# Taking out a 128-byte tile that shifts the feed-forward operand slots against the weights

## The chip, the cores and the metric

The kernel runs on one core of a Trainium2 chip. The metric is the device time of one execution in microseconds (us). Before the change it was 1255.39 us, the median of three runs (1254.78 to 1256.69).

A core has a matrix engine (TensorE, PE in the profile, with its weight loads listed apart as PEld), a vector engine (VectorE, DVE), a scalar engine (ScalarE, ACT), a general one (GpSimd, POOL) and a queue processor (SyncE, SP). Data lies in SBUF, an on-chip memory of 128 partitions; a tile takes the same range of bytes in each of them, so its place is one address. TensorE reads both of its operands from SBUF and writes its sums to another memory, PSUM.

## The reference

The program is a decoder trunk of two layers on 512 tokens of 1,024 channels, in float32, one sequence:

- layer 0 mixes the tokens with attention: 3 groups of 8 heads, causal windows of 128, 512 and 2,048 tokens with strides 1, 4 and 16 and a linear bias, merged by their softmax denominators;
- layer 1 mixes them with causal means over 2, 4, 8 and 16 tokens, each in a quarter of the channels, with a matrix product before and one after;
- each layer then has a feed-forward network, `(silu(h @ gate) * (h @ up)) @ down`, with 2,816 hidden channels;
- there is a root-mean-square norm ahead of each of these and one at the end; the outputs are added to the stream.

## The kernel before

Activations are kept transposed: a tile holds 128 channels on its partitions and the 512 tokens along them (2,048 bytes). A product takes a block of 128 x 128 weights as the stationary operand and streams 512 or 256 columns of activations past it.

**Three products for one.** Each float32 value is split in a rounded part and a remainder (`split`, line 95: `hi` on ScalarE, `lo` on VectorE), both in the type float32r. Every product is then three matmuls, weights hi by activations hi, hi by lo, and lo by hi (lines 272, 273 and 275 in `Product.add`; lines 391 to 393 in `mult`). A pair of hi and lo tiles of 512 columns each, 4,096 bytes together, is what the kernel calls a slot.

**Seven products for eight.** Most of the large products are done by a Strassen scheme of 2 x 2 blocks, with 256 columns to a matmul: `seven` (line 400) and `values12` in attention, `chain` (line 449) in the feed-forward layers. A `chain` goes through its seven block products in a written-out order; each is `n` blocks of 128 by three matmuls. The last of the seven uses a half-size weight tile (`halfhi`, `halflo`) and adds to a sum that was evacuated before. The other products, the "plain" ones, stream all 512 columns: the first five of the 22 hidden blocks of each feed-forward layer (`plain_pair`), the pooling mixer, the output product of attention and some others.

**Where operands lie.** Pools are laid out in SBUF one behind the other. The first, `cpool`, holds the residual stream x, some small tiles and 12 slots; `wpool` holds the raw weights as they land from memory and the split weights; `tmp` holds small temporary tiles. Behind these, one range is used three times over: for the attention pools (`opool`, `apool`), and when they are closed for `fpool` with 16 further slots and, behind it, the scratch pools of the feed-forward layers and of the pooling mixer.

Slots are handed out by a queue. `slot` (line 283) takes the first free number and makes a tile under the tag of that number, in whichever pool the number belongs to; `give` (line 290) puts a number at the queue's end:

```
    free, pools = deque(range(FIXED)), {i: cpool for i in range(FIXED)}

    def slot(name, dtype=F32R):
        i = free.popleft()
        t = pools[i].tile([P, 2, S], dtype, tag=f"slot{i}", name=name, bufs=1)
        return i, t
```

In attention only numbers 0 to 11 exist (`FIXED = 12`); the other operands lie in tiles of the attention pools. When `fpool` opens, numbers 12 to 27 (`SLOTS = 16`) join the queue, and from then on an operand, whatever its name (`h`, `tb`, `tt`, `tn`, `hx`, `hy`, `hz`, `hu`, `n`, `y`), lies in either pool, as the queue has it. Weights always lie in `wpool`, but for those of the pooling mixer's second product (`wg`), which are in slots.

**What sets the order.** One queue of weight loads and one of splits are worked off by `pump` (line 186), which is called between the products, so a split for a later product stands between the evacuations of earlier ones. The order of all instructions is fixed when the program is built, and so is every address.

**Two tiles named shift.** Neither is ever written or read. One, of 256 bytes, is the first of `tmp` (line 89). The other, of 128 bytes, is the first of `fpool` (line 922), ahead of the slots.

Of the kernel before, what the change touches and what calls it, by code (L numbers as in the profile page):

```python
# [8 lines left out]
F32 = mybir.dt.float32  # L9
# [6 lines left out]
P = 128  # L16
# [35 lines left out]
def trunk(ctx: ExitStack, tc: tile.TileContext, xT, norms, w_first, w_qk, w_qkp, w_v0, w_v0p, w_v12, w_out, w_pair, w_down, w_down0, w_down1, w_down2, w_pin, w_pgrp,  # L52
# [866 lines left out]
                note(1, m)  # L919

    with tc.tile_pool(name="fpool", bufs=1) as fpool:
        fpool.tile([P, 32], F32, name="shift", bufs=1)
        for i in range(FIXED, FIXED + SLOTS):
            free.append(i)
            pools[i] = fpool
# [445 lines left out]
```

## Time and profile before

| | |
|---|---|
| median of three runs | 1255.39 us |
| the profiled execution | 1255.31 us, of it 1253.5 us span |
| TensorE (matmuls / weight loads) | 1238.3 us / 1173.6 us busy, 9,072 each |
| VectorE | 1012.8 us busy |
| ScalarE | 679.9 us busy |
| GpSimd | 157.7 us busy |
| granted TensorE clock | 0.998 |
| read from HBM | 186.29 MB, 150 GB/s over the span |

The span is the time between the first and the last instruction that was recorded. Roughly, attention lies in the first 460 us, its output product behind it, the first feed-forward layer from 510 to 835, the pooling mixer and the plain products of the second feed-forward layer from 835 to 957, and the rest of that layer from there to 1242; the norm at the end follows. A matmul's duration in the profile is modelled and reaches into the next one's; what one of them costs in a stream is the distance from its start to the next start.

### The profile page before, as it was taken

The page shows a single profiled execution, that of the slowest core. Times are in us where ns is not written, and L with a number is a line of the kernel's source. Part 1 is how long each engine was busy: PE and PEld are TensorE (multiplying, and loading weights), DVE is VectorE, ACT ScalarE, POOL GpSimd, SP SyncE. Part 2 cuts the span into 40 slices and gives each one's busy share as a digit, 9 for nine tenths or more (in the row PEclk, how much of TensorE's full clock was granted, in tenths as well). Part 3 has the DMA queues.
Part 4 walks back from the last instruction along what each step waited for, and adds up shares of the span by engine and source line. Part 5 has one row for each costly group of instructions (what it writes and reads, how often), then busy time and mean ns, then how long its engine had stood idle before and what let it go on. Part 6 is the DMA issues. An engine that isn't in the chain of part 4 may idle for free. (4 is left out here: it accounts for less than half of the span.)

```text
span 1253.5 us, 23247 instructions
## 1 busy us (share of the span) xinstructions
PE 1238.3 (99%) x9072; PEld 1173.6 (94%) x9072; DVE 1012.8 (81%) x1687; ACT 679.9 (54%) x1171; POOL 157.7 (13%) x147
## 2 busy tenths in 40 slices
PE   9999999999999999999999999999999999999997
PEld 7889999999999998889999999988788999999997
DVE  7987787878778747698778888798989877888876
ACT  6444554445455535466466556554446646656652
POOL 1111111111111010101111111100220111111100
PEclk9999999999999999999999999999999999999999
DMA  8336556655755443437777687553144777677742
GB/s 280 109 92 171 136 143 149 165 133 146 186 141 140 138 152 119 109 94 184 184 186 170 177 191 178 137 198 123 51 118 100 190 189 179 147 192 205 169 123 68
DMA packets 76719, 189.91 MB, mean 151 GB/s; under 512 B 7600, under 2 KB 15936, under 8 KB 76608
## 3 DMA queue, kind: packets, MB, share of 16 engines
q1 hardware_dynamic: 51696, 142.26, 35.8%
q0 software_dynamic: 24336, 45.63, 22.2%
q8 instruction: 71, 1.16, 0.4%
q10 hardware_dynamic: 576, 0.52, 0.1%
q14 instruction: 40, 0.33, 0.1%
HBM read 186.29 MB, written 2.10 MB: 150 GB/s over the span
## 5 line engine op out<-in xcount | busy, mean ns | idle before, releaser
L96 ACT ACTIVATE whi<-raw 128x1024 fp32r<-128x1024 f32 (+2 forms) x315 | 318.7, 1016 | 254.0 <-PE seed L392 78.5
L97 DVE TENSOR_TENSOR wlo<-raw,whi 128x1024 fp32r<-128x1024 f32 (+2 forms) x315 | 366.6, 1167 | 108.0 <-ACT whi L96 107.2
L158 POOL DMA_DIRECT2D raw<-w_pair x34 | 41.1, 1209 | 312.3 <-DMA raw<-w_pair 61.9
L391 PE MATMUL sum<-tt,whi 128*128 128x256 f32 x272 | 77.0, 283 | 1.6 <-ACT seed L473 0.8
L392 PE MATMUL sum<-tt,whi 128*128 128x256 f32 x272 | 76.6, 282 | 0.0
L393 PE MATMUL sum<-tt,wlo 128*128 128x256 f32 x272 | 76.4, 281 | 0.0
L96 ACT ACTIVATE halfhi<-rawhalf 128x512 fp32r<-128x512 f32 (+1 forms) x87 | 53.1, 612 | 19.5 <-PE sum L392 12.2
L173 DVE TENSOR_TENSOR raw<-raw 128x512 f32<-128x512 f32 (+1 forms) x87 | 57.5, 661 | 1.8 <-issue 1.7
L174 DVE TENSOR_TENSOR raw<-raw 128x512 f32<-128x512 f32 (+1 forms) x87 | 57.5, 661 | 0.2
L97 DVE TENSOR_TENSOR halflo<-rawhalf,halfhi 128x512 fp32r<-128x512 f32 (+1 forms) x87 | 57.4, 661 | 0.0
L158 POOL DMA_DIRECT2D raw<-w_down x24 | 28.9, 1206 | 213.8 <-DMA raw<-w_down 75.4
L391 PEld LDWEIGHTS sum<-tt,whi 128*128 128x128 f32 x272 | 51.3, 189 | 2.0 <-ACT seed L473 1.0
L473 ACT COPY seed<-sum 128x256 f32<-128x256 f32 x58 | 20.8, 359 | 57.5 <-PE sum L393 56.3
L392 PEld LDWEIGHTS sum<-tt,whi 128*128 128x128 f32 x272 | 51.3, 188 | 0.0
L393 PEld LDWEIGHTS sum<-tt,wlo 128*128 128x128 f32 x272 | 51.2, 188 | 0.0
L391 PE MATMUL sum<-hz,whi 128*128 128x256 f32 x160 | 45.3, 283 | 0.5 <-ACT seed L473 0.3
L392 PE MATMUL sum<-hz,whi 128*128 128x256 f32 x160 | 45.2, 283 | 0.0
L392 PE MATMUL seed<-hy,whi 128*128 128x256 f32 x160 | 45.2, 282 | 0.0
L393 PE MATMUL seed<-hy,wlo 128*128 128x256 f32 x160 | 45.1, 282 | 0.0
L393 PE MATMUL sum<-hz,wlo 128*128 128x256 f32 x160 | 45.1, 282 | 0.0
L391 PE MATMUL seed<-hy,whi 128*128 128x256 f32 x160 | 45.0, 281 | 0.0
L158 POOL DMA_DIRECT2D raw<-w_qkp x18 | 22.0, 1222 | 166.9 <-DMA raw<-w_qkp 109.4
(610 smaller groups left out, 4628.3 us busy)
## 6 DMA issues: line engine op xcount, KB each, us to landing
raw<-w_pair SPq DMA_DIRECT2D x78, 512.0 KB, 4.8
raw<-w_qkp SPq DMA_DIRECT2D x36, 512.0 KB, 4.3
raw<-w_pair POOLq DMA_DIRECT2D x34, 512.0 KB, 7.7
raw<-w_down SPq DMA_DIRECT2D x32, 384.0 KB, 3.7
raw<-w_v SPq DMA_DIRECT2D x18, 512.0 KB, 4.0
raw<-w_qkp POOLq DMA_DIRECT2D x18, 512.0 KB, 7.3
rawhalf<-w_pair SPq DMA_DIRECT2D x34, 256.0 KB, 4.5
raw<-w_down SPq DMA_DIRECT2D x16, 512.0 KB, 4.7
```

Of the source, the lines that this page charges most:

```text
L96: nc.scalar.activation(hi, v, AF.Copy)
L97: nc.vector.tensor_tensor(lo, v, hi.bitcast(F32), op=OP.subtract)
L158: nc.gpsimd.dma_start(b.rearrange("p (a c) -> p a c", a=2), self.src[:, None, 3 * q:].to_broadcast([P, 2, q]), accum_op=OP.add)
L173: nc.vector.tensor_add(a[:, :q], a[:, :q], b[:, :q])
L174: nc.vector.tensor_add(a[:, q:2 * q], a[:, q:2 * q], a[:, :q])
L391: nc.tensor.matmul(dst, w.t[0][:, c], th, start=k == 0 and not onto, stop=False, skip_group_check=onto)
L392: nc.tensor.matmul(dst, w.t[0][:, c], tl, start=False, stop=False, skip_group_check=onto)
L393: nc.tensor.matmul(dst, w.t[1][:, c], th, start=False, stop=k == n - 1, skip_group_check=onto)
L473: nc.scalar.copy(e, c)
```

## The change

One line goes: the 128-byte tile at the head of `fpool`. The 16 slots and all tiles behind them (the scratch of the feed-forward layers and of the pooling mixer) lie 128 bytes lower. The instructions and their order are the same, and so is the hand-out of slot numbers.

```diff
     with tc.tile_pool(name="fpool", bufs=1) as fpool:
-        fpool.tile([P, 32], F32, name="shift", bufs=1)
         for i in range(FIXED, FIXED + SLOTS):
             free.append(i)
             pools[i] = fpool
```

## The prediction

> **What bounds the kernel now.** I read first the engines' busy time, then busy time stage by stage, then the waits of TensorE, and last the spacing of single matmuls. The first two:
>
> ```profile
> span 1253.5 us, 23247 instructions
> PE 1238.3 (99%) x9072; PEld 1173.6 (94%) x9072; DVE 1012.8 (81%) x1687; ACT 679.9 (54%) x1171; POOL 157.7 (13%) x147
> ...
> 75.00:450.00 375.00, 372.87 (x3030) 367.71 (x3029) 301.87 (x486) 191.78 (x345) 59.22 (x62) 1.00 0.60 153
> 530.00:835.00 305.00, 302.90 (x2399) 295.18 (x2398) 255.35 (x431) 183.76 (x319) 32.79 (x28) 1.00 0.66 166
> 835.00:950.00 115.00, 114.29 (x511) 91.68 (x510) 104.43 (x187) 54.36 (x81) 17.55 (x12) 1.00 0.37 108
> 950.00:1242.00 292.00, 292.00 (x2388) 288.62 (x2387) 237.98 (x413) 173.46 (x306) 32.16 (x27) 1.00 0.64 158
> ```
>
> The columns of the stage rows are time, then busy time with count of PE, PEld, DVE, ACT and POOL, the granted clock, and the DMAs. TensorE is busy throughout: 302.90 of 305.00 us in the first feed-forward layer, 292.00 of 292.00 in the second, always at clock 1.00. DVE has 50 us free in each of these stages. TensorE's waits in the first layer are these, and in the second the view names none:
>
> ```profile
> PE sum L391 <- ACT seed L473: 1.1, 2, 0.8
> PE sum L391 <- ACT seed L465: 1.0, 2, 0.8
> ```
>
> So the time is TensorE's stream of matmuls, and what counts is how far apart two of them start. The durations in the groups (about 280 ns for 256 columns) overlap and don't say that; the starts do. In time order:
>
> ```profile
> 582.31 0.28 PE L391 MATMUL seed<-tn,whi 128*128 128x256 f32 x1
> 582.32 0.19 PEld L392 LDWEIGHTS seed<-tn,whi 128*128 128x128 f32 x1
> 582.43 0.28 PE L392 MATMUL seed<-tn,whi 128*128 128x256 f32 x1
> 582.43 0.19 PEld L393 LDWEIGHTS seed<-tn,wlo 128*128 128x128 f32 x1
> 582.55 0.28 PE L393 MATMUL seed<-tn,wlo 128*128 128x256 f32 x1
> ```
>
> Starts are 0.12 us apart, and the load of the next weights begins with each matmul: TensorE reads two places of SBUF at once, the moving operand in its slot and the next weights. [...]
>
> **The change part by part.** It removes one allocation. No instruction, wait or DMA is added, removed or reordered. The tile is never written. From the tile sizes (small tiles take 32 bytes each) x, the 12 slots of the first pool, raws and weights all lie at one offset modulo 256; the temporary pool is a multiple of 256 long, so the attention pools start at that offset too, and so would the feed-forward pool, but for the 128 bytes. Today the 16 slots there are "displaced" by 128 against the weights; afterwards everything is "aligned". The scratch tiles behind the slots also move by 128 bytes; only DVE, ACT and POOL touch them, and those are hidden by the TensorE stream above (if that cover were gone, nothing in the trace gives them a price by offset).
>
> The trace already holds both layouts. In attention no displaced slot exists, so it is the control. In the feed-forward layers I followed the hand-out of slots through the free list, a queue. Stretches without a stall, 256 columns; the first four wholly aligned (three in attention, one in layer two), the last two wholly displaced:
>
> ```profile
> 98.68:118.71 20.04, 20.04 (x169) 1.00 0.55 131
> 159.66:172.49 12.83, 12.83 (x109) 1.00 0.52 120
> 343.91:350.99 7.08, 7.08 (x60) 1.00 0.66 131
> 1099.19:1104.22 5.03, 5.03 (x44) 1.00 0.46 122
> 640.81:643.66 2.85, 2.85 (x26) 1.00 0.28 106
> 1093.48:1098.12 4.63, 4.63 (x41) 1.00 0.58 101
> ```
>
> The count includes one or two matmuls still running at the left edge; 167, 107, 59, 42, 24 and 39 start inside. Aligned: 20.04/167 = 120.0 ns, 119.9, 120.0, 119.8. Displaced: 2.85/24 = 118.8 and 4.63/39 = 118.7. The aligned stream is the slower one by 1.2 ns, and the last and the fourth row stand next to each other in the same stage, 1 us apart. Why the long aligned runs come so close to 120 is seen just behind a stall in attention; the first row is the eight matmuls that follow it, the second begins two later:
>
> ```profile
> 300.92:301.87 0.95, 0.95 (x10) 1.00 0.88 134
> 302.11:304.99 2.88, 2.88 (x26) 1.00 0.49 87
> ```
>
> 0.95/8 = 118.8 at first, then 2.88/24 = 120.0: an aligned stream settles at 120, a displaced one stays where the aligned one begins. Next, stretches of the feed-forward stages in which the two kinds mix:
>
> ```profile
> 563.59:583.38 19.79, 19.79 (x168) 1.00 0.74 187
> 603.55:613.43 9.87, 9.87 (x85) 1.00 0.73 188
> 786.87:804.56 17.69, 17.69 (x150) 1.00 0.58 139
> 966.18:986.00 19.81, 19.81 (x168) 1.00 0.75 185
> 1086.49:1104.22 17.73, 17.73 (x150) 1.00 0.66 156
> 1104.59:1111.88 7.29, 7.29 (x62) 1.00 0.86 215
> 1187.52:1205.20 17.69, 17.69 (x151) 1.00 0.56 139
> ```
>
> With 167, 83, 149, 167, 149, 61 and 149 starts these are 109.87/925 = 118.8 ns, 118.5 to 119.5 each; the highest, 7.29/61, has the fewest displaced operands (13 of 61). So in the mix even the aligned matmuls run at 118.8: each switch of offset restarts the unsettled phase. After the change there is no switch left, and all of them lose it, not the displaced alone.
>
> Term one. The feed-forward stages hold 4,596 matmuls of 256 columns: per layer 17 block pairs of 7 x 4 x 3 = 84, and down blocks of 4 x 84 + 8 x 63, together 2,268; twice that, and 60 at the end. About 75 of them follow a stall, at present one per 60 matmuls, so the runs will be as long as the third and fourth aligned rows, which I take with a little less for the shorter ones: 119.85. 4,520 x (119.85 - 118.8) = **+4.7 us**. Bounds: 4,596 x (120.0 - 118.8) = +5.5 above, nothing below.
>
> Term two, the wide matmuls (512 columns). Aligned in attention and the start of layer one, then displaced in the pooling stage:
>
> ```profile
> 57.82:68.49 10.66, 10.66 (x48) 1.00 0.36 63
> 462.81:508.86 46.05, 46.05 (x204) 1.00 0.30 92
> 847.01:852.38 5.36, 5.36 (x24) 1.00 0.01 3
> 865.99:870.87 4.88, 4.88 (x22) 1.00 0.64 210
> 879.86:884.75 4.89, 4.89 (x22) 1.00 0.33 107
> ```
>
> With 47 and 203 starts: 226.8 and 226.9 ns. With 23, 21 and 21: 233.0, 232.4, 232.9. Here aligned is the faster one, by 6 ns. Displaced wide operands are 168 of the pooling layer's input h, 60 of n and 12 of y, 240 in all, from 841 to 957 us: 240 x 5.9 = 1.4 at most. Not all stand in such clean runs; I take **-1.3 us** (bounds -1.4 and 0). Wide matmuls are few because only five of 22 hidden blocks and the pooling layer use them; that is why the sign is that of term one.
>
> Term three, small stalls. The last product of a chain often waits some 40 to 100 ns for the evacuation before it:
>
> ```profile
> 583.26 0.28 PE L393 MATMUL seed<-tn,wlo 128*128 128x256 f32 x1
> 583.38 0.33 PE L391 MATMUL sum<-tt,halfhi 128*128 128x256 f32 x1
> 583.54 0.28 PE L392 MATMUL sum<-tt,halfhi 128*128 128x256 f32 x1
> ```
>
> Here the gap is 0.16 instead of 0.12 us. About 60 chains have it. The 12 matmuls in front will take 12 x 1.05 = 13 ns longer; if the evacuation isn't later for that, the stall shrinks by as much: 60 x 13 = 0.8 at most, nothing if it moves along. I take **-0.3 us**.
>
> Sum: +4.7 - 1.3 - 0.3 = +3.1. The profiled execution took 1255.3 us, its span 1253.5 and 1.8 around it; that is at the median of the three runs (1255.39). Forecast **1258.4 us**.
>
> A rule speaks against this. The Trainium skill, "TensorE: Matmul & The Clock Gate", section "Step-by-step: what each phase is for", says of TensorE's two read ports: "Loading the next tile's weights doesn't steal SBUF read bandwidth from the running matmul." By it the offset is worth nothing (the rival below). Its section "Back-to-back issue gap" gives N/2.4 + 2.5 ns, an estimate of 109 and 216 for 256 and 512 columns; the trace has 119 to 120 and 227 to 233, so something beyond streaming is paid here, and it differs with the offset.
>
> **The rivals.** *Ports don't interact* (or the slots don't move by the whole 128): the spacings above differ for another reason, say the stage. Then the time stays at 1255.3; if only the wide ones gain, 1254.0. For it: the 256-column difference is 1%. Against: the two adjacent rows at 1093 and 1099 us.
>
> *Faster*: aligned operands in the feed-forward chains stay in the unsettled, quick phase. There is such a piece, nine aligned matmuls behind a switch:
>
> ```profile
> 602.34:603.39 1.06, 1.06 (x11) 1.00 0.00 0
> ```
>
> 1.06/9 = 117.7 ns. If all ran so, 4,520 x (117.7 - 118.8) - 1.3 = -6.3, 1249 us. It decides from the point where the aligned mean in the two layers lies under 118.5. Against it stand the row from 1099.19 (119.8 in the same stage) and all of attention.
>
> *The whole loss*: stalls no longer unsettle the stream, term one is +5.5, and the wide matmuls, which stand beside other work, gain nothing: 1260.8.
>
> **How the numbers follow.** My forecast has 0.70, ports don't interact 0.15, the whole loss 0.10, faster 0.05. The forecast's own range is 1257.3 to 1259.6 by the bounds of its terms. The range for the time goes from 1254.6, which takes in an unchanged time and most of the small gain, to 1260.6. A measurement of this kernel tells about 0.2% (2.5 us) from no change, that is 1257.9 and above is slower. Of the forecast's 0.70 about 0.51 lies above that and 0.19 below; with the whole loss, slower has 0.61. Same: 0.19 + 0.14 = 0.33. Faster: 0.06, the faster rival and a hundredth of the first.
>
> **What would show it.** In the changed kernel's starts, stall-free stretches of 256 columns after 555 us should average 119.8 to 120.0 and settle at 120 exactly, as attention does; attention and the wide matmuls up to 510 us should not move; displaced wide ones should drop from 233 to 227. The first layer's stage should be some 2 us longer, the second's the same, the pooling stage some 1 us shorter. I am wrong if the 256-column spacing stays near 118.8, if new waits of TensorE of a microsecond appear, or if the pooling stage doesn't shorten.

## The result and the profile after

The changed kernel takes 1257.72 us, the median of 22 runs (1256.51 to 1259.48); the kernel before, over 22 runs, 1255.12 us (1254.11 to 1257.17). The ratio is 1.0019, 95% interval 1.0013 to 1.0024: slower by 0.19%, which is 2.4 us (the two medians differ by 2.6), and lies at the bound of 0.2% that the prediction set itself. The profiled execution has a span of 1256.6 us against 1253.5. Each ratio below is against runs of the kernel before on the same chip.

The head of the page after:

```profile
span 1256.6 us, 23247 instructions
PE 1240.2 (99%) x9072; PEld 1177.5 (94%) x9072; DVE 1012.9 (81%) x1687; ACT 679.8 (54%) x1171; POOL 157.5 (13%) x147
```

VectorE, ScalarE and GpSimd are where they were (1012.8, 679.9, 157.7 before). Only TensorE's numbers grew. Now by stage; the columns are as in the prediction, and each stretch begins and ends at the same matmul in both kernels: the first feed-forward layer, the pooling mixer with the wide products of the second layer, the rest of the second layer. Before:

```profile
515.21:835.08 319.87, 317.77 (x2464) 307.51 (x2463) 270.22 (x456) 192.96 (x333) 35.04 (x29) 1.00 0.66 164
835.08:957.09 122.01, 121.30 (x540) 97.41 (x539) 111.44 (x202) 57.91 (x88) 17.55 (x12) 1.00 0.39 110
957.09:1236.04 278.95, 278.95 (x2308) 276.94 (x2307) 226.39 (x385) 167.04 (x293) 31.34 (x26) 1.00 0.65 162
```

After:

```profile
514.14:835.49 321.35, 319.62 (x2464) 309.74 (x2463) 270.30 (x456) 193.01 (x333) 35.04 (x29) 1.00 0.66 163
835.49:956.53 121.04, 119.93 (x540) 97.30 (x539) 110.98 (x202) 57.74 (x88) 17.50 (x12) 1.00 0.39 111
956.53:1239.13 282.60, 280.92 (x2308) 278.98 (x2306) 226.56 (x386) 167.08 (x294) 31.34 (x26) 1.00 0.65 160
```

The layers got longer by 1.5 and 3.7 us, the wide stage shorter by 1.0. The seven mixed stretches of the prediction, cut at the same matmuls, after the change:

```profile
562.51:582.54 20.03, 20.03 (x168) 1.00 0.75 185
602.82:612.76 9.94, 9.94 (x85) 1.00 0.73 186
787.06:804.93 17.87, 17.87 (x151) 1.00 0.59 136
965.69:985.72 20.02, 20.02 (x168) 1.00 0.73 184
1086.86:1104.73 17.87, 17.87 (x151) 1.00 0.67 152
1105.10:1112.40 7.31, 7.31 (x62) 1.00 0.77 208
1190.27:1208.15 17.87, 17.87 (x151) 1.00 0.54 133
```

167, 83, 149, 167, 149, 61 and 149 matmuls start inside, 925 in all: 110.91/925 = 119.9 ns apart, where it was 118.8. The control in attention and two stretches of the wide matmuls, at the same places as before:

```profile
97.59:117.62 20.03, 20.03 (x169) 1.00 0.54 131
847.42:852.66 5.25, 5.25 (x24) 1.00 0.01 4
866.11:870.87 4.76, 4.76 (x22) 1.00 0.66 223
```

Attention stands still (20.03/167 = 120.0). The wide ones went from 233 to 5.25/23 = 228.2 and 4.76/21 = 226.7.

The order of the matmuls is the same in both kernels, so the distance to the next start can be subtracted matmul by matmul over all 9,072. Wide matmuls are counted as stalled from 245 ns, the others from 150 ns:

| from 515 us on | us |
|---|---|
| 256 columns, unstalled, first layer / second layer | +2.57 / +2.37 |
| 512 columns, unstalled | -1.4 |
| stalled, 256 columns, first layer / second layer | -1.04 / +1.30 |
| stalled, 512 columns | +0.4 |

Attention's first microseconds, which the change doesn't touch, were 1.1 us shorter in this profile. The sum is the 3.1 us by which the spans differ. What the stalls are is taken up behind the experiments.

### The profile page after: what moved, and what is told of

Read it like the earlier page. It is cut to its first block, busy times and chain, and to the rows that moved or that the text cites. A ratio compares the mean times of both kernels' runs of the same rounds, so it can differ in the third digit from the quotient of the medians.

```text
span 1256.6 us, 23247 instructions
## 1 busy us (share of the span) xinstructions
PE 1240.2 (99%) x9072; PEld 1177.5 (94%) x9072; DVE 1012.9 (81%) x1687; ACT 679.8 (54%) x1171; POOL 157.5 (13%) x147
```

## The experiments

My theory: TensorE reads the moving operand and the next weights at the same time, and the spacing of its matmuls follows from the offset of the two places modulo 256. The rivals are that the scratch tiles' new place does it, that the absolute address does, and that it is the switching between two offsets, not the offset.

**Scratch tiles put back.** The padding goes behind the slots.

```diff
-        fpool.tile([P, 32], F32, name="shift", bufs=1)
...
-        invcnt = fpool.tile([P, PAD], F32, name="invcnt", bufs=1)
+        invcnt = fpool.tile([P, PAD + 32], F32, name="invcnt", bufs=1)[:, :PAD]
```

> The changed kernel, with 128 bytes of padding behind the slots, so that the scratch tiles have the addresses of before while the slots stay aligned with the weights. Theory (slots against weights decide): as the changed kernel, 1257.7 us, ratio to before 1.002. Rival (the scratch tiles' new place slows VectorE or ScalarE and through them TensorE): as before, 1255.1, ratio 1.000.

Measured 1258.15 us, ratio 1.0022 (1.0013 to 1.0031). Two of the stretches from above, one with 256 columns (167 starts) and one wide (21):

```profile
563.07:583.09 20.02, 20.02 (x168) 1.00 0.74 185
866.54:871.30 4.76, 4.76 (x22) 1.00 0.71 240
```

119.9 and 226.7 ns, as in the changed kernel. The scratch tiles play no part that these runs can tell.

**256 bytes ahead of the slots.** `[P, 32]` becomes `[P, 64]`.

> The kernel before, with 256 instead of 128 bytes ahead of the slots: slots aligned modulo 256 again, but at another absolute address than in the changed kernel, and off by 256 modulo 512. Theory (only the offset modulo 256 counts): 1257.7 us, ratio 1.002. Rivals: the absolute address or the offset modulo 512 counts, then it is as before, 1255.1; or the removal of the allocation itself costs, then 1255.1 too.

Measured 1258.58 us, ratio 1.0025 (1.0015 to 1.0035). The same two stretches:

```profile
563.20:583.24 20.03, 20.03 (x168) 1.00 0.74 185
865.72:870.48 4.76, 4.76 (x22) 1.00 0.69 226
```

Equal again, with the slots 256 bytes away from where the changed kernel has them. It is neither the absolute address nor the offset modulo 512, and taking the allocation out costs nothing by itself.

**64 bytes ahead of the slots.** `[P, 32]` becomes `[P, 16]`.

> The kernel before, with 64 instead of 128 bytes ahead of the slots. Theory in its narrow form (a switch between two different offsets unsettles the stream, whatever they are): 1255.1 us, ratio 1.000, with 256 columns at 118.8 ns in the feed-forward stages. Rival (128 bytes are special, as half of 256): as aligned, 1257.7. The wide matmuls at 64 bytes may cost another price than at 128, 227 to 233 ns, worth up to 1.4 us.

Measured 1256.04 us, ratio 1.0008 (0.9999 to 1.0017), which doesn't tell it from the kernel before. The same two stretches, and between them one of 149 starts with 256 columns:

```profile
563.46:583.27 19.81, 19.81 (x168) 1.00 0.74 187
787.43:805.19 17.76, 17.76 (x150) 1.00 0.60 139
866.55:871.37 4.82, 4.82 (x22) 1.00 0.64 225
```

118.6, 119.2 and 229.5 ns. Taking the matmuls of the feed-forward stages by slot, those 64 bytes off had 118.1 and the aligned ones between them 120.4, more than they have alone. So a switch doesn't always help the aligned ones; it depends on the pair.

**Matmuls alone.** To have the price of each offset without the kernel around it, a program splits one set of weights and one moving tile as the kernel does and runs streams of the kernel's triples, the moving operand starting `o` bytes on:

```
    def run(n, triples, offs):
        ...
        for k in range(triples):
            e = offs(k) // 4
            c = slice(k % 8 * P, (k % 8 + 1) * P)
            h, l = mhi[:, e:e + n], mlo[:, e:e + n]
            nc.tensor.matmul(p, whi[:, c], h, start=k == 0, stop=False)
            nc.tensor.matmul(p, whi[:, c], l, start=False, stop=False)
            nc.tensor.matmul(p, wlo[:, c], h, start=False, stop=k == triples - 1)
```

> A program of matmuls alone, which computes nothing of the reference: one set of weights, split in hi and lo as in the kernel, is multiplied with one moving tile read from a start that is shifted by 0 to 512 bytes; 72 matmuls of 256 columns for each start, then 36 of 512 columns; also streams in which the start changes every 4 triples or every triple. Theory (the spacing of two starts depends on the moving operand's offset against the weights modulo 256): at shifts 0, 256 and 512 256 columns settle at 120.0 ns and 512 columns at 227; at 128 they take about 118.5 and 232; alternating 0 and 128 gives 118.8. Rival (the offset plays no part, the stage does): all shifts give one and the same spacing. What shifts that are no multiple of 128 give is open.

Streams of 256 columns at 0 (69 starts), 32, 64, 128 and 256 bytes (72 each), then of 512 columns at 0, 64 and 128 (36 each):

```profile
21.13:29.41 8.28, 8.28 (x71) 1.00 0.01 2
37.96:46.35 8.40, 8.40 (x74) 1.00 0.01 2
46.35:54.84 8.48, 8.48 (x74) 1.00 0.00 0
63.46:72.00 8.54, 8.54 (x74) 1.00 0.01 2
97.45:106.08 8.63, 8.63 (x74) 1.00 0.01 2
174.65:182.84 8.19, 8.19 (x38) 1.00 0.01 2
199.58:207.82 8.24, 8.24 (x37) 1.00 0.00 0
216.23:224.63 8.40, 8.40 (x37) 1.00 0.00 0
```

256 columns: 120.0 at 0, 116.7 at 32, 117.8 at 64, 118.6 at 128, 119.9 at 256. 512 columns: 227.5, 228.9, 233.3. The kernel's prices come out here too, where the place of the moving operand is all that differs from stream to stream. Streams that switch between 0 and 128 bytes every four triples came to 119.1 ns, and every triple to 118.8; the first of them (72 starts):

```profile
140.47:149.05 8.58, 8.58 (x74) 1.00 0.01 2
```

Its matmuls at 0 had 119.3, less than the 120.0 that they have alone: this pair does pull the aligned ones down. And neither the aligned place nor the one of before is the best: 32 and 64 are quicker for 256 columns, which most of the kernel has.

**All slots at one offset.** If so, all of cpool's and fpool's slots should get the same offset, in attention too. A tile of W words is put ahead of the weights, and F words stand ahead of the feed-forward slots; the attention pools, which hold wide operands, stay aligned with the weights.

```diff
     wpool = ctx.enter_context(tc.tile_pool(name="wpool", bufs=1))
+    wpool.tile([P, W], F32, name="apart", bufs=1)
...
-        fpool.tile([P, 32], F32, name="shift", bufs=1)
+        fpool.tile([P, F], F32, name="shift", bufs=1)
```

First 128 bytes (W 32, F 32), the test for the switches: every slot is displaced as fpool's were before, and none differs from another.

> The same with 128 in place of 32 bytes: every slot is displaced by 128 bytes against the weights, those of the first pool too, and no switch of offset is left in the feed-forward layers. Theory (displacement itself gives the spacing, 118.6): feed-forward 4,520 x (118.6 - 118.8) = -0.9, attention 2,391 x (118.6 - 119.85) = -3.0, wide +3.4: 1254.7. Rival (only a switch between two offsets unsettles; one offset throughout settles at 120): feed-forward +5, attention 0, wide +3.4: 1263.5.

Measured 1257.37 us, ratio 1.0016 (1.0007 to 1.0025). One feed-forward stretch (167 starts), one of attention (59), one wide (21):

```profile
563.33:583.15 19.82, 19.82 (x168) 1.00 0.75 187
341.89:348.88 7.00, 7.00 (x60) 1.00 0.67 139
865.90:870.78 4.88, 4.88 (x22) 1.00 0.61 214
```

118.7, 118.6 and 232.4 ns. The displaced stream keeps its 118.7 without any switch, so displacement is what counts, and the rival of the switches, which asked for 120 and 1263.5 us, falls. Attention says more: its slots have the addresses of before, and only the weights and what lies behind them have moved. It is the place of the one against the other, not the moving operand's own. The time is 2.7 us above the theory's 1254.7. In the profile attention's unstalled matmuls gained 2.1 us where 3.0 were expected, those of the two layers 0.1 for 0.9, and the stalls of the second layer grew by 2.0. The first of these has a cause that the theory doesn't cover: 666 unstalled matmuls of attention have weights as the moving operand and slots as the stationary one; they are 128 bytes off as well, and stayed at 119.9. Why was not traced.

Then 32 bytes (W 56, F 8) and 64 bytes (W 48, F 16).

> The kernel before, with the slots and the residual stream 32 bytes off the weights modulo 256, all alike, and the attention pools aligned with the weights: a 224-byte tile ahead of the weights, and 32 instead of 128 bytes ahead of the feed-forward slots. Theory (spacing by offset, prices of the first matmul program): 4,520 x (116.7 - 118.8) in the feed-forward stages = -9.5 us, attention 1,719 x (116.7 - 119.85) = -5.4 and 672 with weights as the moving operand x (118.3 - 119.9) = -1.1, wide matmuls +3.4; about 1242.7. Rival (TensorE was held by something else as well, so a faster spacing turns into stalls): 1250 or more. Rival (the program of matmuls alone does not carry over): 1255.

Measured 1248.55 us, ratio 0.9954 (0.9940 to 0.9969). A feed-forward stretch of 149 starts:

```profile
781.95:799.33 17.38, 17.38 (x150) 1.00 0.57 139
```

116.6 ns, as the matmuls alone had. But other stretches settled at 117.8, so that the layers' mean was 117.1, and the stalls took 5.5 us of the gain in the two layers. That is the profiled execution, the slowest of the four (1251.22 us); by the median, half of the expected gain came through.

> The same with 64 bytes: feed-forward 4,520 x (117.8 - 118.8) = -4.5, attention 1,719 x (117.8 - 119.85) = -3.5 and 672 x (117.8 - 119.9) = -1.4, wide matmuls at 228.8 instead of 228 or 232, +0.4 - 0.8 + 0.2: 1245.6. Rival (the program of matmuls alone does not carry over): 1255.

Measured 1245.51 us, ratio 0.9935 (0.9918 to 0.9952), where 1245.6 was expected. Feed-forward (167), attention (59), wide (21):

```profile
557.72:577.39 19.67, 19.67 (x168) 1.00 0.75 188
338.81:345.76 6.95, 6.95 (x60) 1.00 0.70 148
857.48:862.28 4.80, 4.80 (x22) 1.00 0.65 219
```

117.8, 117.8 and 228.6, near the 117.8 and 228.9 of the matmuls alone. That the time came out to 0.1 us is luck in part. The matmuls with weights as the moving operand, which are 192 bytes off in this layout, had 115.0 on the mean where 117.8 was taken (-1.9 us), the layers' unstalled ones gained 1.0 us more than expected, and stalls took some 1.7 us back.

**A finer map.** Two further programs of matmuls alone looked at shifts that aren't multiples of 32.

> The same program of matmuls alone as the first (nothing of the reference is computed), with finer shifts. Theory (the spacing is a function of the offset modulo 256): shift 288 gives the 116.7 ns that 32 gave for 256 columns; shifts between 24 and 48 show how wide the good place is; 512 columns have 233 ns at all of these but for 8 and 72, which are open. Rival (the 116.7 at 32 came from what ran before it): 288 and the alternation give something else, 118 to 120.

The shift 288 gave 116.7 like 32: modulo 256 holds. 8 and 40 gave 120.0, 48 gave 118.3, and 28 and 36, one word to either side of 32, lie at the two ends. Their streams, 72 starts each:

```profile
47.44:55.76 8.32, 8.32 (x74) 1.00 0.00 0
64.16:72.89 8.73, 8.73 (x74) 1.00 0.01 2
```

115.6 and 121.3 ns. There is no smooth curve to be read.

> The program of matmuls alone once more (nothing of the reference is computed), with every shift from 0 to 252 bytes in steps of one 4-byte word: 48 matmuls of 256 columns each, then 24 of 512. Theory: the values of the two earlier programs come again at the shifts they share, 28 stays the best for both widths with 115.5 and 226.7 ns. Open: whether shifts that no earlier run had, such as 60, 92 or 252, are as good, and whether there is a simple rule.

At 28 it was 115.6 and 226.7 again, but no longer the quickest for 256 columns. Over all 64 words the 256-column spacing went from 113.3 to 123.3 ns, the 512-column one from 226.7 to 240.0. Here are 4 and 192 bytes, 48 starts each,

```profile
27.05:32.94 5.90, 5.90 (x50) 1.00 0.00 0
295.94:301.40 5.46, 5.46 (x50) 1.00 0.01 3
```

122.9 and 113.8 with the first few, 123.3 and 113.3 once settled. But not every value came again: 192 had been 117.8 in the first program, 16 was 113.3 where it had been 118.7, and 8 was 116.7 where the second program had 120.0. A rule over the words I did not find.

**Weights one word in.** To use 28, the split weights were cut from strips, one word in, with everything else 32 bytes from the strips' start.

```diff
+AWAY = 1
...
+    wpool.tile([P, 56], F32, name="apart", bufs=1)
...
-    tmp.tile([P, 64], F32, name="shift", bufs=1)
+    tmp.tile([P, 8], F32, name="shift", bufs=1)
...
+    strips = {ring: [wpool.tile([P, BUFS[ring] * COLS[ring] + 64], F32R, name=ring + c, bufs=1) for c in ("hi", "lo")]
+              for ring in ("w", "half")}
...
-                self.t = [wpool.tile([P, n], F32R, tag=ring + c, name=ring + c, bufs=BUFS[ring]) for c in ("hi", "lo")]
+                i = len(rings[ring]) % BUFS[ring]
+                self.t = [t[:, AWAY + i * n:AWAY + (i + 1) * n] for t in strips[ring]]
...
-        fpool.tile([P, 32], F32, name="shift", bufs=1)
```

> The kernel before, with the moving operands 28 bytes off the weights modulo 256 everywhere: the split weights lie in strips from which a tile's worth is cut one word in, and all other pools are at 32 bytes from the strips' start. Theory (prices of the matmul programs carry over): feed-forward 4,520 x (115.6 - 118.8) = -14.5 us, attention 1,719 x (115.6 - 119.85) = -7.3, wide matmuls -1.8, and some 4 us given back as stalls, as in the kernel with 32 bytes: about 1235.5. Rival (weights that start at an odd word slow the splits on VectorE and ScalarE, which are then what TensorE waits for): 1250 or more, with waits of TensorE for the splits. Rival (the quick spacing doesn't carry over): 1255.

Measured 1264.06 us, ratio 1.0072 (1.0058 to 1.0085), where 1235.5 was expected. The products of this layout are not the reference's, so only its spacing is read here. A feed-forward stretch of 149 starts, and the group of the splits:

```profile
790.98:808.86 17.88, 17.88 (x151) 1.00 0.57 142
```

```profile
L99 DVE TENSOR_TENSOR wlo<-raw,whi 128x1024 fp32r<-128x1024 f32 (+2 forms) x315 | 367.4, 1169 | 107.8 <-ACT whi L98 106.4 <-PE sum L398 0.8
```

The splits took 1169 ns on the mean as against 1167 before, and ScalarE's half of them 1017 against 1016: the odd word costs neither anything here, and that rival falls. TensorE's spacing is 120.0, though the offset is 28. So the offset modulo 256 isn't the whole of it: with the odd word on the weights' side the price is another than with it on the moving side. Whether the odd start changes what TensorE reads, and why the products differ, stayed open.

**How a stream is entered.** The two values at 192 bytes ask for a second look: streams whose first 24 matmuls have one shift and the next 72 another.

> The program of matmuls alone (nothing of the reference is computed): streams of 96 matmuls of 256 columns that begin with 24 at one of six shifts and go on with 72 at one of five; each pair once. Theory A (each shift has one spacing to settle at): the 72 have the same mean whatever came first: 120.0 at 0, 118.7 at 16, 117.8 at 64, 118.6 at 128, 117.8 at 192. Theory B (a stream locks in one of several phases, and which one hangs on how it was entered, as 113.3 and 117.8 at shift 192 and 113.3 and 118.7 at shift 16 in the earlier programs suggest): at 0 always 120, at some of the others two or more values, among them 113.3.

Theory B. At 0 the 72 went to 120.0 from each of the six, at 128 to 118.5 to 118.7. At 16 they went to 118.7, but from 32 to 116.7; at 64 and at 192 either to 117.8 or to 113.3. At 192, entered from 64 and from 128 (71 spacings each):

```profile
329.56:337.62 8.05, 8.05 (x73) 1.00 0.00 0
340.58:348.94 8.36, 8.36 (x73) 1.00 0.01 2
```

113.4 and 117.7 ns for the same addresses. Entered from 0 it was 113.3, and from 192 itself 117.8; which entry leads where has no pattern that I could name.

**All slots at 192 bytes** (W 16, F 48).

> The kernel with all slots at 192 bytes from the weights modulo 256 (the layout of the runs with 32, 64 and 128 bytes). Theory A (117.8 ns at 192, as first measured): feed-forward 4,520 x (117.8 - 118.8) = -4.5 us, attention 1,719 x (117.8 - 119.85) = -3.5 and 672 x (117.8 - 119.9) = -1.4, wide matmuls +3.4: 1249. Theory B (the quick phase of 113.3 is entered often, as in the kernel with 64, where the 672 with weights as the moving operand took 115.0): some 10 to 20 us less, 1230 to 1240.

Measured 1240.93 us, ratio 0.9890 (0.9874 to 0.9907): 14 us quicker than the kernel before, the quickest of all, and just above the range that theory B gave. A feed-forward stretch (149), attention (59), wide (21):

```profile
777.40:794.31 16.91, 16.91 (x150) 1.00 0.59 137
339.03:345.73 6.70, 6.70 (x60) 1.00 0.70 150
855.80:860.71 4.90, 4.90 (x22) 1.00 0.66 230
```

113.5 and 113.6 ns, with wide matmuls at 233.3. The quick phase is the one that the feed-forward layers mostly found (114.2 on the mean); attention's operands found it less often (115.9). TensorE has become quick enough that others show: the stalls of the two layers took 8 of the 20 us that the spacing gained.

## Why the prediction was right, and where it was off

- **What bounds the kernel**: right. The other engines' times didn't move with the offset, and 3.5 us of unstalled spacing came through as 2.4 to 3.1 us of time.
- **Term one**, +4.7: the trace has +2.57 and +2.37, together +4.9. The spacing came to 119.9 where 119.85 was taken. It grew in aligned and displaced matmuls alike, as said. That all matmuls of the mix ran at 118.8 was read as unsettling by each switch; this reason is only half right. The stretches at 128 bytes throughout show that the displaced ones have 118.7 of their own, and the mix with 64 bytes shows aligned ones at 120.4. What is lost with the change is the displaced place itself and, with this pair, the aligned ones' share in it.
- **Term two**, -1.3: the trace has -1.4, from 233 to 227, in the stage named. The count of 240 leaves out 24 matmuls whose `y` lies in the first pool and whose weights `wg` lie in `fpool`; these were displaced as well, and at 5.9 ns each they are worth 0.1 us.
- **Term three**, -0.3, was too small. Between 130 and 300 ns the feed-forward stages had 75 stalls with 5.3 us over 120 ns before, and 63 with 3.9 us after: -1.4. With the other two repeats of the aligned layout it was -1.5 and -1.6. So the shrinking was right in its sign, and the bound of 13 ns a stall, 0.8 in all, was too tight. The step that failed is the 12 matmuls: the evacuation follows a matmul further back. In the prediction's example it is held up behind a split, and the split's first half on ScalarE follows a matmul that started at 580.29 us, 26 matmuls ahead of the stalled one:

```profile
580.61 1.06 ACT L96 ACTIVATE whi<-raw 128x1024 fp32r<-128x1024 f32 x1 [0.89 <-PE seed L392]
581.70 1.23 DVE L97 TENSOR_TENSOR wlo<-raw,whi 128x1024 fp32r<-128x1024 f32 x1 [1.93 <-ACT whi L96]
582.85 0.42 DVE L1074 TENSOR_TENSOR up<-sum,half 128x256 f32<-128x256 f32 x1
```

Taking 35 stalls of this kind in the two layers one by one, the time from the start of the matmul 24 places earlier to the end of the stall is the same before and after to 0.5 ns on the mean, while from 12 places earlier it is 11.6 ns less after the change. Each of the 35 shrank by 27 ns on the mean, twice the 13 allowed.
- **The sum**: +4.9 - 1.4 - 1.4 = +2.1, and long stalls of 0.6 to 2 us that come and go: 1.9 us in the profile before, 3.4, 2.9 and 0.7 us in the three of the aligned layout. One of the prediction's signs of being wrong is among them, a new wait of TensorE of over a microsecond. The kind that grew was 1.0, 2 and 0.8 before; after:

```profile
PE sum L391 <- ACT seed L465: 2.3, 3, 1.7
```

The longest of these three waits stands at 1132 us. The copy that TensorE waits for (L465) is behind a split on ScalarE that waits for its weights from memory; the first two lines are from the kernel before, the last two from the changed one:

```profile
1128.86 1.06 ACT L96 ACTIVATE whi<-raw 128x1024 fp32r<-128x1024 f32 x1 [1.47 <-DMA raw<-w_pair]
1130.34 0.37 ACT L465 COPY seed<-sum 128x256 f32<-128x256 f32 x1
1131.94 1.06 ACT L96 ACTIVATE whi<-raw 128x1024 fp32r<-128x1024 f32 x1 [3.96 <-DMA raw<-w_pair]
1133.42 0.36 ACT L465 COPY seed<-sum 128x256 f32<-128x256 f32 x1
```

That load took 9.1 us from issue to landing, where the median of its kind is 7.9. With the scratch tiles put back the same split waited 3.56 us and TensorE stalled at the same place; with 256 bytes ahead of the slots there was no such stall. So this one is a late load. Whether the change makes such loads more frequent is not shown; three executions of the aligned layout and one of the kernel before are too few.

Forecast 1258.4, measured 1257.72. The missing 1.1 us of term three would alone put it at 1257.3; what brings it back up lies among term one's 0.2 and the long stalls, which no term had, so the nearness is luck in part. The range that the forecast gave itself, 1257.3 to 1259.6, can't be had from the bounds of its terms either. The chance for slower than 0.2% was put at 0.61 with the threshold at 1257.9; the median stopped just short of it.
- **The rivals.** *Ports don't interact* fell: the same instructions with the same weights need 113.3 to 123.3 ns at 256 columns, by where the moving operand lies and by what ran before, and moving the weights and not the slots changed attention's spacing from 119.8 to 118.6. The sentence quoted from the Trainium skill's "TensorE: Matmul & The Clock Gate", section "Step-by-step: what each phase is for", that loading the next weights doesn't steal bandwidth from the running matmul, is not borne out by this stream; that it is the reading ports that meet is argued, as no run left the weight loads out. The gap of N/2.4 + 2.5 ns, which the prediction took from the section "Back-to-back issue gap" of the same page of the Trainium skill, is given there for an isolated matmul and not for a stream with a weight load each, so the step from it to "something beyond streaming" has no support there. *Faster* as described fell, for no aligned stream stays in the quick phase: at 0 bytes each of six entries led to 120.0. *The whole loss* fell with term two.
- **The stages**: the pooling stage was 1.0 us shorter and the first layer 1.5 us longer, as said. "The second's the same" held for the unstalled matmuls (+2.37); the stage as a whole grew by 3.7, with 1.3 of it in stalls.

## What to carry to other kernels

Where TensorE is busy all the time, measure the distance between the starts of its matmuls, not their durations, and compare places of the trace that differ in one thing only; that gave the price of the spacing before the change was made, +4.7 and -1.3 us where +4.9 and -1.4 were measured. The place of the moving operand against the weights, modulo 256 bytes, is worth some 5% of a stream of 256-column matmuls in float32r (113.3 against 120.0 ns), and the aligned place is good for 512 columns and poor for 256 (226.7 and 120.0). Try a few multiples of 32 bytes on the chip, give all operands the same one, and expect a part of the gain back as stalls.

## What the runs showed of the hardware that was not expected

- A stream of 256-column float32r matmuls with a weight load each settles at a spacing that goes with the offset: 120.0 ns at 0 and 256 bytes, 116.7 at 32, 117.8 or 113.3 at 64 and 192, 118.7 at 128. For 512 columns it is 226.7 at 0, 228.9 at 64, and 233.3 at 32, 128 and 192.
- Some offsets have several settled spacings, and what ran before decides: at 192 bytes 113.4 after a stretch at 64, 117.7 after one at 128; at 16 bytes the programs show 113.3, 116.7 and 118.7.
- Places one word apart can differ by much of the whole range: 115.6 at 28 bytes, 116.7 at 32, 121.3 at 36.
- With the weights one word past a multiple of 32 bytes and the moving operand 28 bytes on, the spacing was 120.0 and not 115.6, so the offset alone does not give the price; nor does it where weights are the moving operand, 119.9 at 128 bytes in attention. VectorE's splits to and from these odd words took the same 1169 ns (1167 before).
- A move of VectorE's and ScalarE's scratch tiles by 128 bytes changed nothing that the runs could tell: 1258.15 us with them put back, 1257.72 without.
